# Issuing two memory-to-memory cache copies at another point of a hybrid attention and mLSTM layer

## The chip, the cores and the metric

The kernel runs on one core of one Trainium2 chip. The metric is the device time of one execution in microseconds (us). Three runs of the kernel before took 1609.83, 1607.42 and 1612.91 us, with a median of 1609.83. Beside them stands one profiled execution, from which every duration below is taken.

## The reference

One layer of a streaming model takes 256 prompt tokens and 64 sample tokens, each 2048 wide. The sample tokens attend to 512 cached keys and values. All numbers are float32. Cut to what is computed:

```
z = x @ w_in                                   # x 320 x 2048, w_in 2048 x 7184
attn: softmax(q k^T / 8 + bias) v, 16 heads, head norm
      sample: keys = [cache_k (512), new keys (64)], the same for values
      new_k_sample = [cache_k, k][-512:]       # 448 cached rows stay, 64 are new
      new_v_sample = [cache_v, v][-512:]
mLSTM: conv, gates, 8 heads of 128, head norm, * sigmoid(o)
x1 = layer_norm(alpha * x + concat(attn, mLSTM) @ w_out)
y  = layer_norm(alpha * x1 + (silu(x1 @ w_gate) * (x1 @ w_up)) @ w_down)
```

Of each of the two sample outputs, rows 0 to 447 are rows 64 to 511 of the cache, unchanged. These 448 rows of 1024 float32 are 1.84 MB for the keys and as much for the values. No engine computes on them: a DMA reads them from device memory and writes them to device memory.

## The kernel before

**Weights.** All matrices are cut into pieces of 512 KB (128 partitions x 1024 float32, mostly four blocks of 128 rows by 256 columns). `load_piece` (line 98) issues one DMA per piece on the queue of SyncE (SP), into one of four `raw` buffers. `split_piece` makes of it a high part on ScalarE (ACT, line 124, `hi`) and a low part on VectorE (DVE, line 125, `lo`); there are three buffers of each. TensorE (PE) then runs three passes per block (lines 174, 175, 177), which is 24 matmuls per piece of 256 columns. `run_plan` walks the list of pieces: it loads up to three pieces ahead and splits up to two ahead. Pieces are numbered here from 0; the first four make up the first strip of `w_in`.

**The opening.** The input `x` comes in four quarters (`xq`), each issued on SP just ahead of one of pieces 0 to 3. PE transposes each quarter (line 209), ACT and DVE split the result (`xhi`, line 210; `xlo`, line 211). Piece n multiplies quarter n. On ACT the high part of piece 4 stands ahead of the last quarter's `xhi`. After that quarter PE transposes the two tiles of small parameters (lines 234 and 235), and then runs piece 3.

**GpSimd's queue.** POOL issues the other DMAs: small parameters; a table of biases `fdram` (line 267); the cached keys and values that attention reads (`u`, lines 303 and 304, 512 KB each, into memory that the last two quarters of `x` held, so that they wait for their transposes); bias rows `tz` (line 312, 144 KB each); the mLSTM's states `cn` (line 584, 64 KB each, into the buffers of the small parameters, so that they wait for line 235). Between the static fills (line 289) and these loads, the program issues the two copies of the cache rows that stay (line 940).

**What sets the order.** Only the opening's PE, ACT and DVE work runs in the order of the text. Everywhere else a scheduler orders each engine's instructions by its own estimate of when their inputs will be there; an instruction without an input to wait for can be put far ahead of its place in the text. Each engine runs its list strictly in that order. POOL's DMAs take eight completion semaphores in turn, and each DMA waits until the last one with its semaphore has landed.

Of the kernel before, what the change touches and what calls it, by code (L numbers as in the profile page):

```python
# [23 lines left out]
SS = 64  # L24
T = SP + SS
PAST = 512
# [8 lines left out]
TOK = [(0, 128), (128, 128), (256, 64)]  # L35
# z columns
QA, KA, VA, QR, KR, VB, OB, IB = 0, 1024, 2048, 3072, 4096, 5120, 6144, 7168
# conv buffer: 3 past | prompt | 3 past | sample
CP0, CS0, CW = 3, 262, 326
# [4 lines left out]
class Piece:  # L44
    """A slice of a weight matrix and what is done with it."""

# [14 lines left out]
def _build(tc, nc, I, O, es):  # L61
# [12 lines left out]
    V, S, G, TE = nc.vector, nc.scalar, nc.gpsimd, nc.tensor  # L74

    # ---------------------------------------------------------------- input x
    xq = []
# [11 lines left out]

    # ------------------------------------------------------- weight streaming  # L90
    plan = []
    raws = []
    loaded = []
# [8 lines left out]
    def split_piece(between=None):  # L102
        i = len(loaded)
        pc, raw = plan[i], raws[i]
        raws[i] = None
        n = pc.nk * pc.ncol
        hi = wp.tile([P, PIECE], F32R, tag="hi", bufs=3, name="hi")
        if pc.perm:
            lo = None
            r3 = raw[:, 0:n].rearrange("p (k c) -> p k c", k=pc.nk)  # L110
            h3 = hi[:, 0:n].rearrange("p (k c) -> p k c", k=pc.nk)
            # high and low parts of the gates' columns side by side, for one pass with both
            S.copy(h3, r3)
            for d0, s0 in ((0, 112), (32, 120)):
                S.copy(h3[:, :, d0:d0 + 8], r3[:, :, s0:s0 + 8])
                V.tensor_tensor(out=h3[:, :, d0 + 64:d0 + 72], in0=r3[:, :, s0:s0 + 8],
                                in1=h3[:, :, d0:d0 + 8].bitcast(F32), op=ALU.subtract)
        else:
            lo = wp.tile([P, PIECE], F32R, tag="lo", bufs=3, name="lo")
            for j, m in enumerate((0, n // 2) if between else (0,)):  # L120
                if j:
                    between()
                cs = slice(m, m + n // 2 if between else n)
                S.copy(hi[:, cs], raw[:, cs])  # L124
                V.tensor_tensor(out=lo[:, cs], in0=raw[:, cs], in1=hi[:, cs].bitcast(F32),  # L125
                                op=ALU.subtract)
        loaded.append((hi, lo))
# [68 lines left out]

    # ------------------------------------------------------------ x transposed
    xhi = big.tile([P, KT, T], F32R, tag="A", bufs=2, name="xhi")
# [14 lines left out]

    # -------------------------------------------------------------- mixer pool
    mctx = tc.tile_pool(name="mx", bufs=1)
    mx = mctx.__enter__()

    # parameters that go along the partitions
    pcol = const.tile([P, P], F32, name="pcol")
# [28 lines left out]
    def rsqrt(out, u, n, m, tag):  # L248
        """out = u ** -0.5 by Newton's iteration; u and out are [n, m] in SBUF."""
        pool = const  # L250
# [8 lines left out]

    # ------------------------------------------------- relative position bias  # L260
    fdram = dp.tile([HA, 640], F32, name="fdram")
# [6 lines left out]

    # ------------------------------------------------------------- mix storage
    mixbuf = {}  # L270
# [8 lines left out]

    # ---------------------------------------------------------------- attention  # L280
    qbd = [const.tile([P, 5, P], F32, name="qbd%d" % i) for i in range(2)]
# [11 lines left out]
    def attn_loads(u):  # L293
        a = {}
# [4 lines left out]
        a["pT"] = u1[:, 1024:2432].rearrange("p (n c) -> p n c", c=P)  # L299
        # the second pair's probabilities take the place of the cached keys, then dead  # L300
        a["pt"] = [((0, u2[:, 1024:2240]),), ((960, u2[:, 2240:2496]), (0, u1[:, 0:960]))]
# [39 lines left out]
    def attn_gen(u, i):  # L341
        a = attn[u]
# [3 lines left out]
        cs = slice(i * P, (i + 1) * P)  # L346
        # keys and values by token, cached keys by feature
        for srcs, dst in ((vT, vtok), (kT, ktok)):
# [17 lines left out]
        yield  # L366
        # scores: cached keys | new keys, c1, c3, c0 | c2
        sa, sb, sc = w_tile(), w_tile(), w_tile()
# [25 lines left out]
        yield  # L394
        # probabilities by key
        pT = a["pT"]
# [57 lines left out]

    # -------------------------------------------------------------------- gates
    gate = {}
# [16 lines left out]
    def gates_done(ps):  # L473
# [9 lines left out]
        V.tensor_tensor(out=ig, in0=ig, in1=z[64:72, 0:T], op=ALU.add)  # L483
        # log_sigmoid(f) = min(f, 0) - log(1 + exp(-|f|))
        V.scalar_tensor_tensor(out=e, in0=f, scalar=-1.0, in1=f, op0=ALU.mult, op1=ALU.min)
# [16 lines left out]
        G.dma_start(out=gd_m, in_=nM)  # L502
        # exp(g - M_L), scaled as the keys need it
        wk = t8("ig2")
        for a, b in SEG:
            S.activation(wk[:, a:b], g[:, a:b], AF.Exp, bias=nM[:, b - 1:b])
        V.tensor_scalar(st[32:40, :], wk, KSC, None, ALU.mult)
        # exp(-m_t) = exp(-M - F)
        e1 = t8("e1")
        V.tensor_tensor(out=e1, in0=nM, in1=F, op=ALU.subtract)  # L510
        S.activation(e1, e1, AF.Exp)
        V.tensor_copy(st[64:72, :], e1)
        # exp(m_in - M), halved for the doubled queries
        wi = mx.tile([HB, SS], F32, tag="g8_wi", name="wi")
# [25 lines left out]

    # -------------------------------------------------------------------- mLSTM
    ml = {}
# [4 lines left out]
    def qk_done(u, kind, ps):  # L547
        for i in range(2):
# [14 lines left out]
            S.activation(th, acc, AF.Tanh, scale=0.5)  # L563
            # twice the SiLU
            y = mx.tile([P, CO], F32, tag="conv" + kind, bufs=2, name="cy")
# [11 lines left out]
    def mlstm_gen(h, i):  # L577
# [65 lines left out]
        G.tensor_copy(nnw[:, :, h], cw[:, :, 128])  # L643
        # h = num / max(|den|, exp(-m)), then the head's norm
        d = mx.tile([P, 3], F32, tag="d", bufs=2, name="d")
# [45 lines left out]
    def state_rows():  # L691
        """Rows of the conv and normaliser states, from the columns that were kept."""
        ps = w_tile()
# [9 lines left out]

    # ------------------------------------------------------ plan of the w_in part
    W = I["w_in"]
# [23 lines left out]

    # ------------------------------------------------------------- w_out and LN1  # L730
    def mix_rhs(k):
# [31 lines left out]
    def stat_gen(s, keep):  # L763
        """Token-major copies of two feature tiles of y: their statistics, and for the last
        norm the values too."""
        y, st = late["y"], late["st"]
# [22 lines left out]
    def sqrt_table(after):  # L789
        """Has the square root's table loaded before the norm's chain needs it."""  # L790
        d = const.tile([P, 1], F32, tag="sqd", name="sqd")
        S.activation(d, after, AF.Sqrt, bias=eps, scale=0.0)

    def norm_stats():
        """Mean and variance of the tokens, in columns for the three token tiles."""
        st = late["st"]
# [6 lines left out]
    def norm_rsqrt(mv):  # L803
# [5 lines left out]
        V.reciprocal(rn, sd)  # L809
        # one step of Newton's iteration  # L810
        a = const.tile([P, 3], F32, tag="rna", name="rna")
# [8 lines left out]

    # ----------------------------------------------------------------------- FFN
    x1 = {}
# [3 lines left out]

    # the first unit takes y * g with the columns g and b beside it; its norm is applied to
    # the products: W'((y - mu) r g + b) = r W'(y g) - mu r W'g + W'b
    def yg_rhs(k):
# [67 lines left out]
    def gate_up(u):  # L897
# [3 lines left out]
        if u == 0:  # L901
            # done with each quarter of the rows early, for the normed ones to replace them
            for pa, pb in zip(a, b):
                plan.extend((pa, pb))
        else:
            plan.extend(a + b)
# [16 lines left out]

    # --------------------------------------------------------------- the program
    for q in range(4):
# [12 lines left out]
    mix_tiles()  # L938
    for nm in ("k", "v"):
        G.dma_start(out=O["new_%s_sample" % nm][0:PAST - SS, :], in_=I["cache_attn_" + nm][SS:PAST, :])  # L940

    run_plan(n_in)
# [9 lines left out]
    G.dma_start(out=late["g2"], in_=ln2["g"].to_broadcast([P, DM]))  # L952
    # rows g, g, g, b, b as high, low, high, high, low parts
    gr = lp.tile([5, DM], F32, name="gr")
# [11 lines left out]

    # first norm, by feature
    def x1_gen():
# [21 lines left out]
        for c in range(KT):  # L990
            # in place of the rows that the first unit is done with
            if c % 2 == 0:
# [8 lines left out]
            V.tensor_tensor(out=lo, in0=y[:, c, :], in1=hi.bitcast(F32), op=ALU.subtract)  # L1001

    run_plan(len(plan))
    flush()

    # second norm, by token
    with tc.high_priority():
        for _ in stat_gen(7, (late["ytp"], late["yts"])):
# [5 lines left out]
                               op0=ALU.mult, op1=ALU.mult)  # L1014
        # rows -mean * r as high, high, low parts and ones, for -mean * r * g + b
        c5 = lp.tile([P, 3, 5], F32, name="c5")
# [55 lines left out]
```

## Time and profile before

| What | Value |
|---|---|
| median of three runs | 1609.83 us |
| span of the profiled execution (from its first to its last instruction; the profile gives no other time of it) | 1611.0 us |
| TensorE, share of the span | 98% |
| VectorE, ScalarE, GpSimd | 52%, 39%, 8% |
| mean granted TensorE clock | 0.990 |
| DMA, mean over the span | 148 GB/s |
| DMA, first fortieth of the span | 301 GB/s |

Each row of the tables is one group, wait or instruction; times within the span count from its start. In rows of the timeline the first number is the start, the second the duration, and the bracket at the end is the idle time of that engine just before, with what ended it. In the views of the DMA queues, q1 is the queue that SP fills and q0 the one that POOL fills; the row gives packets, MB and the share of the 16 DMA engines' time that the packets took.

### The profile page before, as it was taken

What the parts mean: (1) busy time and instruction counts of PE and PEld (TensorE: products, weight loads), DVE (VectorE), ACT (ScalarE), POOL (GpSimd) and SP (SyncE); (2) the same over time, 40 slices, a digit from 0 to 9 for tenths busy, and PEclk for the clock granted to TensorE, in tenths of its full rate; (3) what the DMA queues carried; (4) which work ended last, traced back from release to release, by engine and by line L of the source; (5) the groups of instructions that cost most, each with busy time, mean ns of one, the idle gap of its engine ahead of it and who ended that gap; (6) DMA issues with size and microseconds to landing.
All of it is one profiled execution on the core that took longest, in us unless ns stands there. A gap on an engine that the chain in (4) does not pass through costs nothing.

```text
span 1611.0 us, 26591 instructions
## 1 busy us (share of the span) xinstructions
PE 1579.4 (98%) x10906; PEld 1549.3 (96%) x10906; DVE 836.8 (52%) x1512; ACT 632.3 (39%) x972; POOL 123.4 (8%) x254
## 2 busy tenths in 40 slices
PE   5999999999999999999999999999999999999997
PEld 4999999999999999899999999999999999999996
DVE  3477585575665755853444444344444434444456
ACT  3356445444444533543333233333333333333332
POOL 3021111101000100400000000000000000000004
PEclk9999999999999999999999999999999999999997
DMA  9455444444344544354444444444444444444441
GB/s 301 152 158 153 144 144 147 149 144 128 121 128 128 176 142 143 105 169 145 151 150 148 154 145 155 145 155 146 148 153 146 156 144 154 148 150 151 148 141 66
DMA packets 225545, 238.99 MB, mean 148 GB/s; under 512 B 8683, under 2 KB 219819, under 8 KB 225227
## 3 DMA queue, kind: packets, MB, share of 16 engines
q1 hardware_dynamic: 220384, 220.23, 43.3%
q0 software_dynamic: 5040, 17.07, 3.3%
q8 instruction: 85, 1.39, 0.4%
q14 instruction: 36, 0.29, 0.1%
HBM read 230.85 MB, written 10.07 MB: 150 GB/s over the span
## 4 chain that ended last, share of the span: by engine, by line
PE 95%; DVE 2%; DMA 2%; issue 0%; ACT 0%; DVEq 0%; SPq 0%; ACTq 0%
PE mm L174 30%; PE mm L177 29%; PE mm L175 29%; DMA raw<-w_in 2%; PE w L419 1%; DVE lo L125 1%; PE w L771 1%; PE w L375 0%; PE w L399 0%; PE w L614 0%; DVE ytp L1034 0%; PE w L402 0%; PE w L352 0%; PE w L358 0%; PE w L377 0%; DVE t L998 0%
## 5 line engine op out<-in xcount | busy, mean ns | idle before, releaser
L125 DVE TENSOR_TENSOR lo<-raw,hi 128x1024 fp32r<-128x1024 f32 (+1 forms) x409 | 501.0, 1225 | 606.4 <-ACT hi L124 606.3
L124 ACT CAST hi<-raw 128x1024 fp32r<-128x1024 f32 (+1 forms) x409 | 428.1, 1047 | 754.8 <-PE mm L175 650.8
L177 PE MATMUL mm<-x1h,lo 128*128 128x320 f32 (+1 forms) x1408 | 436.5, 310 | 2.2 <-DVE lo L125 2.2
L174 PE MATMUL mm<-x1l,hi 128*128 128x320 f32 (+1 forms) x1408 | 435.6, 309 | 0.9 <-DVE np L844 0.9
L175 PE MATMUL mm<-x1h,hi 128*128 128x320 f32 (+1 forms) x1408 | 435.6, 309 | 0.0
L174 PE MATMUL mm<-xlo,hi 128*128 128x320 f32 x912 | 289.1, 317 | 0.0
L175 PE MATMUL mm<-xhi,hi 128*128 128x320 f32 x912 | 282.0, 309 | 0.0
L177 PE MATMUL mm<-xhi,lo 128*128 128x320 f32 x896 | 278.3, 311 | 0.5 <-DVE lo L125 0.5
L177 PEld LDWEIGHTS mm<-x1h,lo 128*128 128x128 f32 x1408 | 265.8, 189 | 2.6 <-DVE lo L125 2.5
L174 PEld LDWEIGHTS mm<-x1l,hi 128*128 128x128 f32 x1408 | 265.6, 189 | 1.3 <-DVE np L844 1.2
L175 PEld LDWEIGHTS mm<-x1h,hi 128*128 128x128 f32 x1408 | 265.4, 189 | 0.0
L174 PE MATMUL mm<-hl,hi 128*128 128x320 f32 x704 | 218.0, 310 | 0.0
L177 PE MATMUL mm<-hh,lo 128*128 128x320 f32 x704 | 217.5, 309 | 0.0
L175 PE MATMUL mm<-hh,hi 128*128 128x320 f32 x704 | 217.5, 309 | 0.0
L174 PEld LDWEIGHTS mm<-xlo,hi 128*128 128x128 f32 x912 | 172.4, 189 | 2.2
L175 PEld LDWEIGHTS mm<-xhi,hi 128*128 128x128 f32 x912 | 172.6, 189 | 0.0
L177 PEld LDWEIGHTS mm<-xhi,lo 128*128 128x128 f32 x896 | 169.4, 189 | 0.8 <-DVE lo L125 0.8
L175 PEld LDWEIGHTS mm<-hh,hi 128*128 128x128 f32 x704 | 132.2, 188 | 0.0
L174 PEld LDWEIGHTS mm<-hl,hi 128*128 128x128 f32 x704 | 132.1, 188 | 0.0
L177 PEld LDWEIGHTS mm<-hh,lo 128*128 128x128 f32 x704 | 132.1, 188 | 0.0
L779 POOL TENSOR_TENSOR ytp<-ytp,g 128x256 f32<-128x256 f32 x16 | 13.6, 875 | 894.6 <-ACT ytp L776 894.6
L888 DVE SCALAR_TENSOR_TENSOR y<-y,mm 128x320 f32<-128x320 f32 x96 | 46.5, 484 | 48.9 <-PE mm L177 48.6
(313 smaller groups left out, 1344.5 us busy)
## 6 DMA issues: line engine op xcount, KB each, us to landing
raw<-w_in SPq DMA_DIRECT2D x114, 512.0 KB, 3.5
raw<-w_ffn_gate SPq DMA_DIRECT2D x88, 512.0 KB, 3.5
raw<-w_ffn_up SPq DMA_DIRECT2D x88, 512.0 KB, 3.5
raw<-w_ffn_down SPq DMA_DIRECT2D x88, 512.0 KB, 3.3
raw<-w_out SPq DMA_DIRECT2D x32, 512.0 KB, 3.3
tz<-fdram POOLq DMA_DIRECT2D x16, 144.0 KB, 2.9
xq<-x_prompt SPq DMA_DIRECT2D x4, 512.0 KB, 8.6
u<-cache_attn_k POOLq DMA_DIRECT2D x4, 512.0 KB, 6.2
```

The source lines that it names most:

```text
L124: S.copy(hi[:, cs], raw[:, cs])
L125: V.tensor_tensor(out=lo[:, cs], in0=raw[:, cs], in1=hi[:, cs].bitcast(F32), op=ALU.subtract)
L174: TE.matmul(o, hi[:, sl], xl, start=st, stop=False)
L175: TE.matmul(o, hi[:, sl], xh, start=False, stop=en and pc.perm)
L177: TE.matmul(o, lo[:, sl], xh, start=False, stop=en)
L419: TE.matmul(ox[r, c * 64:(c + 1) * 64], pT[0:n, j, r], src[0:n, k, v0:v0 + 64], start=(m == 0), stop=(m == len(terms[c]) - 1))
L771: TE.transpose(dst[j][:, i * P:(i + 1) * P], y[:, 2 * s + i, t0:t0 + n], ident)
L779: G.tensor_tensor(out=keep[0][:, j, cs], in0=keep[0][:, j, cs], in1=late["g2"][:, cs], op=ALU.mult)
L888: V.scalar_tensor_tensor(out=y[:, c, :], in0=y[:, c, :], scalar=ALPHA if g == 0 else 1.0, in1=ps[i][:, 0:T], op0=ALU.mult, op1=ALU.add)
```

## The change

The loop that issues the two copies is taken from its place after `mix_tiles()` and put between two calls of `run_plan` in the feed-forward part: the plan now runs up to 32 pieces past the end of `w_out`, then come the copies, then the rest of the plan. The other differences of the file are comments that are gone, and shifted line numbers: lines 943 to 1001 are three lower in the changed kernel, those behind one higher, and the copies stand on line 1003.

```diff
     mix_tiles()
-    for nm in ("k", "v"):
-        G.dma_start(out=O["new_%s_sample" % nm][0:PAST - SS, :], in_=I["cache_attn_" + nm][SS:PAST, :])
-
     run_plan(n_in)
     flush()
     state_rows()
...
+    run_plan(n_out + 32)
+
+    for nm in ("k", "v"):
+        G.dma_start(out=O["new_%s_sample" % nm][0:PAST - SS, :], in_=I["cache_attn_" + nm][SS:PAST, :])
     run_plan(len(plan))
     flush()
```

What the scheduler makes of it is seen in the engines' lists. This is POOL's list of the kernel before, in the opening, from the last static fill (`vt1`) on: `u1` and `u2` are the cached keys and values that attention reads.

```order
L289 MEMSET vt1_87 128x3
L940 DMA new_k_sample<-cache_attn_k 32x14336
L940 DMA new_v_sample<-cache_attn_v 32x14336
L303 DMA u1_379<-cache_attn_k 128x4x256
L304 DMA u2_380<-cache_attn_v 128x4x256
L312 DMA tz_383<-fdram_81 64x576 x2
L312 DMA tz_386<-fdram_81 64x576 x2
L553 MEMSET craw_874 128x3
L494 MEMSET gst_1258 128x320
L584 DMA cn_1499<-state_mlstm_C 128x128
L584 DMA cn_1564<-state_mlstm_C 128x128
```

The same place in POOL's list of the changed kernel, from the last of six fills (lines 553, 494, 648 and 649) that now follow `vt1`:

```order
L649 MEMSET ss_1784 128x3
L1003 DMA new_k_sample<-cache_attn_k 32x14336
L303 DMA u1_377<-cache_attn_k 128x4x256
L304 DMA u2_378<-cache_attn_v 128x4x256
L312 DMA tz_381<-fdram_81 64x576 x2
L312 DMA tz_384<-fdram_81 64x576 x2
L584 DMA cn_1497<-state_mlstm_C 128x128
L584 DMA cn_1562<-state_mlstm_C 128x128
L1003 DMA new_v_sample<-cache_attn_v 32x14336
L312 DMA tz_1616<-fdram_81 64x576
```

The copies have no input to wait for, and the scheduler has put both into the opening again. The copy of the keys stands where it stood, behind six fills instead of ahead of them; the copy of the values has moved behind the loads of `u2`, `tz` and `cn`, and so behind the wait of `cn` for line 235. SP's list, which holds all loads of weights, is the same in both kernels.

PE's list changes in the first attention unit only. In the kernel before, the second head pair of that unit starts like this (352 and 353 are transposes of new values and keys, 358 of cached keys, 174 to 177 matmuls of the strips):

```order
L352 MATMUL w<-ident,vT 128x128 x2
L353 MATMUL w<-ident,vT 64x128
L174 MATMUL mm<-xlo,hi 128x320
L175 MATMUL mm<-xhi,hi 128x320
L177 MATMUL mm<-xhi,lo 128x320
L174 MATMUL mm<-xlo,hi 128x320
L352 MATMUL w<-ident,kT 128x128 x2
L353 MATMUL w<-ident,kT 64x128
L175 MATMUL mm<-xhi,hi 128x320
L177 MATMUL mm<-xhi,lo 128x320
L358 MATMUL w<-ident,u_379 128x128 x4
```

In the changed kernel the same place reads:

```order
L352 MATMUL w<-ident,vT 128x128 x2
L353 MATMUL w<-ident,vT 64x128
L352 MATMUL w<-ident,kT 128x128 x2
L353 MATMUL w<-ident,kT 64x128
L358 MATMUL w<-ident,u_377 128x128 x4
```

The strip's matmuls come behind the transposes instead of between them; units 1 to 3 have this second order in both kernels. ACT's and DVE's lists change in the same unit, and from there to the end no engine's list differs in more than line numbers.

## The prediction

> **What bounds the kernel now.** I read the page first, then PE's waits, then the chain of waits over the opening, then the two DMA queues by stretches. The page's first lines:
>
> ```profile
> span 1611.0 us, 26591 instructions
> PE 1579.4 (98%) x10906; PEld 1549.3 (96%) x10906; DVE 836.8 (52%) x1512; ACT 632.3 (39%) x972; POOL 123.4 (8%) x254
> ```
>
> PE is idle for 1611.0 - 1579.4 = 31.6 us, so no change of waits can win more, apart from what the clock gives. The list of PE's waits (us in total, times, longest) says where most of that lies:
>
> ```profile
> PE w L234 <- DVE xlo L211: 11.3, 1, 11.3
> PE w L1024 <- DVE c L1021: 5.4, 1, 5.4
> PE w L209 <- DMA xq<-x_prompt: 5.4, 1, 5.4
> PE mm L177 <- DVE lo L125: 2.7, 2, 2.2
> ```
>
> The second is the tail, the third the first load of `x`, and the fourth never exceeds 2.2 us. The change is near the first: one wait of 11.3 us in the opening. PE's timeline says when it began, and the chain of waits (start, us, what) what stands behind `xlo`:
>
> ```profile
> 28.40 0.31 PE L177 MATMUL mm<-xhi,lo 128*128 128x320 f32 x1
> ```
>
> ```profile
> 10.81 26.31 DMA raw<-w_in
> 37.23 1.05 ACT hi L124
> 38.30 1.23 DVE lo L125
> ...
> 39.98 0.47 PE w L234
> 40.46 0.28 PE w L235
> 40.74 0.56 PE mm L174
> 41.30 0.27 PE mm L175
> ...
> 44.22 0.15 PE mm L174
> ```
>
> PE's last matmul of piece 2 ends at 28.40 + 0.31 = 28.71, and the next instruction starts at 39.98: 11.27 us. The load of piece 4, issued at 10.81, took 26.31 us and landed at 37.12; its high part, which on ACT stands ahead of the last `xhi`, follows, and 2.86 us after the landing PE starts. So a stretch of a kernel that is PE-bound elsewhere is **bound by one DMA**. What held it is in the two queues; two rows each over 10 to 19 us and over 19 to 29 us, and one over 37 to 42 us:
>
> ```profile
> q1 hardware_dynamic: 2152, 2.75, 104.5%
> q0 software_dynamic: 203, 0.07, 4.2%
> q0 software_dynamic: 89, 3.69, 97.5%
> q1 hardware_dynamic: 126, 0.13, 4.0%
> q1 hardware_dynamic: 1396, 1.39, 95.0%
> ```
>
> From 10 to 19 us the loads from SP had the engines nearly alone (2.75 MB against 0.07). From 19 to 29 us POOL's queue moved 3.69 MB, which is the two copies (2 x 1.84), and the weights got 0.13 MB in 10 us. With POOL's queue nearly empty, from 37 to 42 us, they got 1.39 MB in 5 us, 0.278 MB per us. Between those, from 29 to 37 us, both queues moved:
>
> ```profile
> q0 software_dynamic: 452, 1.54, 63.1%
> q1 hardware_dynamic: 689, 0.68, 36.1%
> ```
>
> 1.54 + 0.68 = 2.22 MB in 8 us is the same 0.278 MB per us, two thirds of it for the attention's loads (`u` 2 x 0.52, `tz` 4 x 0.15 MB by their shapes). POOL's instructions show why these came so late:
>
> ```profile
> 14.52 0.51 POOL L940 DMA_DIRECT2D new_k_sample<-cache_attn_k  x1
> 15.03 0.51 POOL L940 DMA_DIRECT2D new_v_sample<-cache_attn_v  x1
> 21.20 0.80 POOL L303 DMA_DIRECT2D u<-cache_attn_k  x1 [5.66 <-PE w L209]
> 27.05 0.77 POOL L304 DMA_DIRECT2D u<-cache_attn_v  x1 [5.06 <-PE w L209]
> 27.81 2.16 POOL L312 DMA_DIRECT2D tz<-fdram  x4
> 40.76 1.10 POOL L584 DMA_DIRECT2D cn<-state_mlstm_C  x2 [10.38 <-PE w L235]
> ```
>
> ```profile
> new_k_sample<-cache_attn_k POOLq DMA_DIRECT2D x1, 1792.0 KB, 10.4
> new_v_sample<-cache_attn_v POOLq DMA_DIRECT2D x1, 1792.0 KB, 15.9
> ```
>
> The second fence is from the list of DMA issues: the copies landed 10.4 and 15.9 us after their issue, at 24.9 and 30.9: one behind the other, with about 5 us of the ten for each. The attention's loads queue behind both.
>
> **The change, part by part.** By POOL's list the change doesn't take the copies to the feed-forward part. It moves one of them, by a few instructions.
>
> *Keys.* Its copy stays ahead of `u`. Six fills come before it, one of which took 0.42 us and the others about what the last did:
>
> ```profile
> 29.95 0.42 POOL L494 MEMSET gst<- 128x320 f32 x1
> 41.94 0.13 POOL L649 MEMSET ss<- 128x3 f32 x1
> ```
>
> They overlap, so I add 0.7 us: it is issued at 15.2 instead of 14.52, and its 5 us run from 19.7 to 24.7.
>
> *Values, taken out.* The 5 us from 24.7 on are free. Up to about 29 only the first `u` (issued at 21.20, 0.52 MB) competes: the second is issued at 27.05, and POOL waits there for PE, not for the queue. Piece 4 lacks at most its whole 0.52 MB at 24.7. If the weights go first, it lands 0.52 / 0.278 = 1.9 us later, at 26.6; if `u` goes first, 3.7 us later, at 28.4. The other end lets every later load keep its place ahead of the weights; then the landing moves only by the copy's own 5 us, from 37.12 to 32.1. I take **28.5**, the case of `u` first, because the second `u` and `tz` can't move before they are issued, and their issue times come from PE. PE then starts at 28.5 + 2.86 = 31.4, its gap is 31.4 - 28.71 = 2.7 us, and 11.3 - 2.7 = **8.6 us** go (5.0 with the landing at 32.1, and 10.5 with it at 26.6).
>
> *The clock.* Once the opening is over, ACT splits a piece every 3.52 us, in PE's rhythm:
>
> ```profile
> 52.91 1.05 ACT L124 CAST hi<-raw 128x1024 fp32r<-128x1024 f32 x1 [2.47 <-PE mm L175]
> 56.43 1.05 ACT L124 CAST hi<-raw 128x1024 fp32r<-128x1024 f32 x1 [2.47 <-PE mm L175]
> ```
>
> That is 3.52 / 24 = 0.147 us per matmul. Behind the gap they are 0.27 us apart (the chain above): from 40.74 to 44.22 PE did 12 of them in 3.48 us instead of 1.76: **1.7 us** lost. When the clock fell is told by the row of a stretch (busy times, then the granted clock, the DMA share, GB/s):
>
> ```profile
> 33.00:35.00 2.00, 0.00 (x0) 0.00 (x0) 0.00 (x0) 0.00 (x0) 0.00 (x0) 0.71 1.07 334
> ```
>
> The slow rate is half the full one (0.27 to 0.147), and a mean of 0.71 between 1 and 0.5 means that it fell 0.84 us into this stretch, at 33.8, 5.1 us after PE stopped. A gap of 2.7 us stays under that, so I count the 1.7 us as won; with a gap over 5.1 us nothing of it is won. [...]
>
> *Values, put back.* This copy now waits behind `cn`, so for line 235. `cn` was issued 0.78 us after PE's restart and two take 1.10 us, so the copy is issued at 31.4 + 1.9 = 33.3. The copy of the keys moved its first data about 4.5 us after its issue (14.52 to 19, up to which POOL's queue moved only 0.07 MB), which gives 37.8 to 42.8 for this one, and in that time weights get almost nothing. What covers it is pieces in hand. From 28.5 to 37.8 the engines move 9.3 x 0.278 = 2.59 MB; the second `u`, `tz` and `cn` (2 x 0.07) take 1.24, and 1.35 MB are left, 2.6 pieces: 5, 6 and half of 7. PE needs 3.52 us per piece. From 31.4 + 0.8 on, pieces 3, 4, 5 and 6 keep it busy until 46.3; piece 7 must have landed 2.3 us (`hi` and `lo`) before, at 44.0. Its rest of 0.21 MB after 42.8 takes 0.8 us: 43.6. So it is just in time. If the cover fails altogether, it costs the 5 us; if not, nothing. I take **0.3**, near nothing, because the sum comes out in time, though barely. [...]
>
> *What is queued behind it.* The next instruction on POOL is a `tz`, which before stood idle until 85.43:
>
> ```profile
> 85.43 0.53 POOL L312 DMA_DIRECT2D tz<-fdram  x1 [43.37 <-DVE mxs L386]
> ```
>
> So nobody waits for a later issue, nor for the second `cn`, which now also waits for the keys' landing, long past.
>
> *The new order of attention unit 0.* Cost 0, since units 1 to 3 have that order already. Of equal stretches, that of unit 0 holds as many matmuls as that of unit 1, and PE is never idle in either:
>
> ```profile
> 74.00:124.00 50.00, 50.00 (x406) 47.70 (x405) 35.66 (x113) 26.33 (x59) 9.00 (x22) 1.00 0.50 152
> 189.00:239.00 50.00, 50.00 (x406) 47.79 (x405) 36.61 (x110) 23.35 (x51) 8.88 (x22) 1.00 0.49 152
> ```
>
> The bounds are 0 and 2.2 us, the longest wait of line 177 on `lo`.
>
> *The sum*: 1611.0 - 8.6 - 1.7 + 0.3 = 1601.0. The span lies 1.2 us above the runs' median of 1609.83, so a median of **1600** us is forecast.
>
> **The rivals.**
>
> A. *The gap shrinks only by the copy's own 5 us.* For: the attention's loads did take two thirds of the engines from 29 to 37. Against: their issue times don't move. The gap is 6.3 us, the clock falls, and the time is 1609.8 - 5.0 = 1604.8.
>
> B. *The clock halves sooner.* The gap is some 4 us and the clock falls in it: 7.3 us won, no 1.7, and 0.3 given back: 1602.8. For: one fall can't tell how the idle time is counted. Against: it took 5.1 us in the only long gap between matmuls. [...]
>
> C. *The copy of the values starves PE once it is moved.* It begins earlier than reckoned, before piece 6 is in hand, and PE waits its whole 5 us; with the clock kept, 1600 + 4.7 = 1604.7, and to 1606.4 with a second drop of the clock. For: the margin is 0.4 us.
>
> D. *Slower: the same, with a starvation as long as this copy's whole flight.* At `cn`, weights stand still for the 15.9 us that it took to land before, against 7.0 us (two pieces) in hand: 8.9 us of waiting and 1.7 of slow clock, beside a gain of only 5.0 as in A: 1609.8 + 5.6 = 1615.4. It is slower than before from a standstill of 10.3 us on (5.0 + 7.0 - 1.7). Against: 5 of those 15.9 us were the other copy's, and more was spent behind other loads.
>
> E. *Both copies leave the opening, as the text of the change has it.* Then the gap and the slow clock go: 1609.8 - 13.0 = 1596.8, if two copies amid the feed-forward part hide. POOL's list says otherwise.
>
> **How the numbers follow.** Forecast 0.55, A 0.15, B 0.11, C 0.12, D 0.04, E 0.03. The range 1596 to 1606 takes in all but D and the worst of C, with the spread of the runs. About 0.3%, 4.8 us, is what a measurement of this kernel can tell from no change. Faster by more: forecast, B, E and half of A, 0.77; within: C and the other half of A, 0.19; slower: D, 0.04.
>
> **What would show it.** Right: PE's wait at line 234 falls from 11.3 to 2 to 4 us; the load of piece 4 lands near 28.5; line 1003 shows two issues, near 15 and 33 us; no matmul at 0.27 us behind the gap; no new wait for `lo` from 35 to 50 us. Wrong: a copy issued in the feed-forward part, a gap over 5 us, or a PE wait on `raw` between 40 and 50 us.

## The result, and the profile after

| | before | after |
|---|---|---|
| median of four runs each, side by side | 1609.32 us (1607.42 to 1612.91) | 1601.93 us (1600.72 to 1603.01) |
| ratio, 95% interval | | 0.9949 (0.9935 to 0.9964) |
| span of the profiled execution | 1611.0 us | 1599.2 us |

The changed kernel is 7.4 us faster by the medians (0.46%); the ratio puts the gain at 0.51% (0.36 to 0.65). By the two profiled spans it is 11.8 us. These numbers differ because of which executions were profiled: every run of this kernel takes 1.7 to 2.1 us more than its span, so the profile of before belongs to a run of about 1612.9 us, the slowest of its four. That of after belongs to one of 1601.19.

The first two lines of the page of after:

```profile
span 1599.2 us, 26591 instructions
...
PE 1577.6 (99%) x10906; PEld 1547.5 (97%) x10906; DVE 836.4 (52%) x1512; ACT 631.9 (40%) x972; POOL 122.9 (8%) x254
```

PE's idle time fell from 31.6 to 1599.2 - 1577.6 = 21.6 us, by 10.0, and its busy time by 1.8. Both are in the opening. PE's waits of after (us in total, times, longest):

```profile
PE w L1025 <- DVE c L1022: 5.4, 1, 5.4
PE w L209 <- DMA xq<-x_prompt: 5.4, 1, 5.4
PE mm L177 <- DVE lo L125: 2.7, 2, 2.2
PE w L234 <- DVE xlo L211: 1.1, 1, 1.1
```

The wait ahead of line 234 fell from 11.3 to 1.1 us. The other rows stand as they stood. One short wait joins them: 0.2 us for a `hi` at 9.33 us, before either copy is issued, so it is not the copies' doing. The chain of waits through the opening of after (start, us, what):

```profile
11.50 15.55 DMA raw<-w_in
27.15 1.06 ACT hi L124
28.23 1.23 DVE lo L125
29.46 0.41 DVE xlo L211
29.92 0.33 PE w L234
30.24 0.19 PE w L235
30.44 0.34 PE mm L174
30.78 0.15 PE mm L175
```

Piece 4 is there at 11.50 + 15.55 = 27.05 us instead of 37.12, and PE starts 2.87 us later. Behind the gap the matmuls come at 0.15 us, not at 0.27: the slow clock is gone too. POOL's timeline of after (start, us, engine, line, operation; in brackets the idle time before and what ended it):

```profile
15.33 0.51 POOL L1003 DMA_DIRECT2D new_k_sample<-cache_attn_k  x1
...
30.54 1.10 POOL L584 DMA_DIRECT2D cn<-state_mlstm_C  x2 [0.49 <-PE w L235]
31.62 0.52 POOL L1003 DMA_DIRECT2D new_v_sample<-cache_attn_v  x1
```

Both copies are in the opening, at 15.33 and 31.62. Their packets show in the two queues of after, from 19 to 24 us, from 24 to 25.5, from 24 to 29, and from 37 to 42 (packets, MB, share of the 16 engines; two rows for each stretch):

```profile
q0 software_dynamic: 32, 1.84, 90.8%
q1 hardware_dynamic: 310, 0.31, 19.4%
q1 hardware_dynamic: 365, 0.36, 75.9%
q0 software_dynamic: 15, 0.00, 0.6%
q1 hardware_dynamic: 1066, 1.06, 66.8%
q0 software_dynamic: 160, 0.52, 29.3%
q0 software_dynamic: 49, 1.33, 66.0%
q1 hardware_dynamic: 224, 0.23, 13.6%
```

The first two rows are the copy of the keys, 32 packets of 57 KB, with 0.31 MB of weights in the same stretch. Of these, 0.29 MB passed before 20 us, while the large packets were only starting; from 20 to 24.2 us it was 16 packets of 1 KB, beside the 16 large ones that started then. The next four are the five microseconds that the change frees: 1.06 MB of weights beside the first `u` of 0.52, with the weights alone up to 25.5 us. In the last two the copy of the values does to the weights what that of the keys did, but nobody waits for them by then. That is seen in PE's waits from 30 to 70 us (one row, which is the end of the gap above) and in ACT's timeline:

```profile
43.99 1.05 ACT L124 CAST hi<-raw 128x1024 fp32r<-128x1024 f32 x1 [5.05 <-DMA raw<-w_in]
45.46 1.05 ACT L124 CAST hi<-raw 128x1024 fp32r<-128x1024 f32 x1 [0.42 <-DMA raw<-w_in]
...
48.13 1.05 ACT L124 CAST hi<-raw 128x1024 fp32r<-128x1024 f32 x1 [1.23 <-PE mm L175]
```

ACT waits 5.05 us for piece 8, and from 48.13 on it waits for PE again, as in the steady part. PE takes a piece every 3.52 us from 30.44 on and so comes to piece 8 at about 48.0, which is an estimate. Piece 8 is split about 2.3 us after 43.99, at 46.3. So 1.7 us were to spare.

### The profile page after: what moved, and what is told of

Its sections match the earlier page's. It is cut to its first block, busy times and chain, and to the rows that moved or that the text cites. A ratio compares the mean times of both kernels' runs of the same rounds, so it can differ in the third digit from the quotient of the medians.

```text
span 1599.2 us, 26591 instructions
## 1 busy us (share of the span) xinstructions
PE 1577.6 (99%) x10906; PEld 1547.5 (97%) x10906; DVE 836.4 (52%) x1512; ACT 631.9 (40%) x972; POOL 122.9 (8%) x254
## 4 chain that ended last, share of the span: by engine, by line
PE 95%; DVE 2%; DMA 1%; issue 0%; SPq 0%; ACT 0%; DVEq 0%; ACTq 0%
PE mm L174 30%; PE mm L177 30%; PE mm L175 29%; PE w L419 1%; DMA raw<-w_in 1%; PE w L771 1%; DVE lo L125 1%; DMA xq<-x_sample 1%; PE w L375 0%; PE w L399 0%; PE w L614 0%; DVE ytp L1035 0%; PE w L352 0%; PE w L402 0%; PE w L358 0%; PE w L377 0%
```

## The experiments

The theory: the whole gain is the gap ahead of line 234 with the slow clock behind it; taking either copy out from between 19 and 30 us is enough; where it goes costs nothing as long as the pieces in hand last. The rivals: the gain is the spread of runs; it is due to the new order in attention unit 0 or to a true move into the feed-forward part; the moved copy takes back a part. Three chips served, one for each group of runs, and every ratio is to runs of before on the same chip.

### Before again, and one copy moved at a time

The kernel before, run again as if it were a change:

> The kernel before once more, to see how far its own gap in front of line 234 moves from run to run. Theory (the gap is set by the two copies in front of piece 4, and its length varies with how the packets fall): the ratio's interval contains 1, the gap lies between 6 and 12 us, and the runs scatter by some 4 us. Rival (the gap is fixed, and the runs scatter for another reason): the gap is 11.3 us again within 0.5 us, whatever the time.

Measured: 1612.13 us (1604.51 to 1614.42, 10 runs), ratio 1.0004 (0.9989 to 1.0019). Its profiled execution, of 1610.04 us and a span of 1608.1, has another gap than the one shown with the prediction. Of its chain of waits:

```profile
11.47 22.62 DMA raw<-w_in
34.19 1.05 ACT hi L124
...
36.95 0.47 PE w L234
```

Its DMA queues over 9 us of the copies, from 19.75 to 28.75 us, and behind them those of the kernel before that the prediction showed, from 19.5 to 28.5:

```profile
q0 software_dynamic: 64, 2.75, 84.6%
q1 hardware_dynamic: 64, 0.07, 2.1%
q0 software_dynamic: 64, 2.75, 83.7%
q1 hardware_dynamic: 64, 0.06, 2.2%
```

Piece 4 landed at 34.09 instead of 37.12, and the gap is 7.6 us (its wait row says so too). So **the gap of before is not a constant**, and before scatters over 9.9 us here while after stayed within 2.9 in its ten runs, four beside the result and six with the last pair below. But once the large packets run, the counts are the same in both profiles: 64 packets of POOL's queue (48 of them of 57 KB) and 64 of weights. What differs is what had passed by then and how fast the loads came after it: the first large packet started at 19.48 us here and at 19.03 in the other, and by 34 us 4424 packets had passed in SP's queue instead of 4330. At the 57 to 83 packets a microsecond that passed there from 33 to 36 us, those 94 packets are some 1.5 us (an estimate). The rest of the 3.0 us between the two landings stays open.

Only the copy of the values moved:

```diff
-    for nm in ("k", "v"):
+    for nm in ("k",):
         G.dma_start(out=O["new_%s_sample" % nm][0:PAST - SS, :], ...)
...
+    run_plan(n_out + 32)
+    for nm in ("v",):
+        G.dma_start(out=O["new_%s_sample" % nm][0:PAST - SS, :], ...)
```

> Only the copy of the values is taken to the later place in the text; the copy of the keys stays in its place, ahead of the six fills. In POOL's list the values' copy again comes behind cn. Theory (the whole gain is the values' copy leaving the front of piece 4): PE's wait at line 234 is 1 to 3 us, the slow matmuls behind it are gone, and the time is that of the changed kernel within 2 us. Rival (moving the keys' copy behind six fills, or the new order of attention unit 0, has a share): less than three quarters of the gain.

Measured: 1602.22 us (1600.14 to 1603.14), 0.9944 (0.9927 to 0.9961), a gap of 2.15 us and no slow matmul behind it. It does what the change does. The mirror of it, with only the copy of the keys moved:

> Mirror of the one before: only the copy of the keys is moved, the copy of the values stays in front. Theory (it matters only that one copy of two stands in front of piece 4, not which): the same wait of 1 to 3 us at line 234 and the same time as the changed kernel within 2 us. Rival (the keys' copy collides with the attention's load of the cached keys, or the order of the two matters): the wait stays above 5 us.

Measured: 1601.17 us (1599.61 to 1604.76), 0.9943 (0.9923 to 0.9963). It doesn't matter which copy stays. The profiled execution of this run is the slowest of its four runs, and holds a surprise. The gap is 2.97 us and PE starts again at 32.02. Two stretches of 3.41 us (busy us of PE, PEld, DVE, ACT, POOL, the granted clock, the DMA share, GB/s):

```profile
29.67:33.09 3.42, 1.07 (x6) 0.89 (x7) 2.75 (x6) 2.89 (x6) 1.49 (x5) 1.00 1.10 348
33.09:36.50 3.41, 3.41 (x15) 3.41 (x14) 1.86 (x7) 0.83 (x2) 1.29 (x7) 0.50 1.04 218
```

The clock fell at 33.09, when PE had been at work for a microsecond, and 0.27 us per matmul lasted until 36.5. More on this below.

### No copy in the opening

The copies left out:

> Both copies are left out, so rows 0 to 447 of the two sample outputs stay unwritten. Theory (after the change only about 1 us of the gap is left to win, and the moved copy costs nothing): the wait at line 234 is 0 to 1.5 us and the time is within 2 us of the changed kernel. Rival (the copy that stays in front, or the moved one, still costs several us): 3 us or more below the changed kernel.

Measured: 1600.73 us (1600.26 to 1601.05), 0.9937 (0.9921 to 0.9952), and no wait at line 234 at all. This is what can be had by moving the copies: after, which did not run beside it, is 1.2 us above it. Next, the copies at the point that the change's text names. They are held there until GpSimd's last operation of the first norm is done:

```diff
-            G.tensor_tensor(out=t1, in0=y[:, c, :], in1=mu, op=ALU.subtract)
+            late["last"] = G.tensor_tensor(out=t1, in0=y[:, c, :], in1=mu, op=ALU.subtract)
...
-    for nm in ("k", "v"):
-        G.dma_start(out=O["new_%s_sample" % nm][0:PAST - SS, :], ...)
...
+    run_plan(n_out + 32)
+    with tc.issue_after(late["last"].ins):
+        for nm in ("k", "v"):
+            G.dma_start(out=O["new_%s_sample" % nm][0:PAST - SS, :], ...)
```

> What the text of the change says: both copies are held, by an edge in the scheduler, behind the last of line 997's subtractions on POOL, and so are issued in the feed-forward part, near 680 us. Theory (10 us of large packets there are covered by three pieces in hand, but barely): the opening's gap is 0 to 1.5 us, PE waits 0 to 4 us for a piece in the feed-forward part, and the time is within 4 us of the changed kernel. Rival (steady weight traffic has no slack): PE waits 8 us or more there and the gain is mostly gone.

Measured: 1601.95 us (1601.21 to 1602.11), 0.9934 (0.9914 to 0.9955). They are issued at 670.2 and 670.7. Its queues from 671 to 683 us, and PE's only wait from 670 to 700:

```profile
q0 software_dynamic: 96, 3.67, 87.6%
q1 hardware_dynamic: 255, 0.26, 7.7%
```

```profile
PE mm L174 <- DVE np L844: 2.4, 1, 2.4
```

The weights get 0.26 MB in 12 us there, and PE waits for none of them; its one wait is for VectorE's part of the norm. That wait is 0.9 us in the profiles of before and after, and 2.5 in a second profile of the changed kernel (the run again, below), which has no copy there; so its length varies without the copies. By these times a true move is worth no more than the one that the scheduler made.

### How long a standstill is hidden

Both copies held behind the load of the states, where after has one:

```diff
+        ld = G.dma_start(out=cn[:, 0:128], in_=I["state_mlstm_C"][h])
+        if h == 1:
+            late["cn"] = ld
...
+    with tc.issue_after(late["cn"].ins):
         for nm in ("k", "v"):
```

> Both copies are held behind the second cn on POOL, where the changed kernel has only that of the values. Theory (in the changed kernel the moved copy's five us of standstill used up nearly all pieces in hand, since ACT waited 5.05 us for a piece and PE 0.2): twice the standstill costs PE 3 to 7 us between 40 and 55 us, so the time lies 2 to 6 us above the changed kernel's. Rival (there is more slack): PE waits under 1 us there, and the time equals the changed kernel's.

Measured: 1602.44 us (1600.59 to 1603.11), 0.9936 (0.9918 to 0.9955). The wait that was expected did not come. (The 0.2 us of PE's waiting that the expectation counted is the wait at 9.33 us, ahead of the copies.) Its large packets ran from 33.1 to 44.9 us, and the row of that stretch (length, then busy us of PE, PEld, DVE, ACT, POOL, the granted clock, the DMA share, GB/s) is

```profile
33.00:45.00 12.00, 12.00 (x83) 12.00 (x83) 3.68 (x3) 4.01 (x5) 0.00 (x0) 1.00 1.01 377
```

PE was busy for all of the 12 us. With the front free, the loads had run ahead, and the pieces in hand were more than had been counted. Where the cover ends was still open, so a third copy, of the cached keys into scratch memory, went ahead of these two:

```diff
+        scr = dp.tile([PAST - SS, 1024], F32, name="scr")
+        G.dma_start(out=scr, in_=I["cache_attn_k"][SS:PAST, :])
         for nm in ("k", "v"):
```

> As in the run with both copies behind the states' load, with a third copy of 1.84 MB of the cached keys into scratch memory issued just ahead of them, so that a standstill of the weights three copies long stands in one piece. In the run with two, the large packets ran from 33.1 to 44.9 us, piece 9 landed at 45.4 and was split by about 50.1, and TensorE, which needed it at about 50.5, did not wait. A third copy takes 5 to 6 us more. Theory 1 (the copies cost nothing only while pieces in hand last): the large packets end at 50 to 51 us, piece 9 lands near 51, TensorE waits 4 to 6 us for hi or lo at 50 to 56 us, 14 to 24 matmuls behind it run at the slow clock (2 to 3 us), and the time is 5 to 9 us above that run: 1607 to 1611. Theory 2 (copies behind cn are hidden whatever their length, since the loads of weights still get their share): no new wait, within 1.5 us of 1602.

Measured: 1607.73 us (1605.36 to 1610.97, 10 runs), 0.9977 (0.9965 to 0.9989). PE's waits from 30 to 75 us, and of the stretches behind them two rows:

```profile
PE mm L174 <- ACT hi L124: 5.4, 1, 5.4
PE mm L177 <- DVE lo L125: 0.4, 1, 0.4
```

```profile
46.00:48.00 2.00, 0.65 (x5) 0.39 (x3) 0.00 (x0) 0.00 (x0) 0.00 (x0) 1.00 0.39 118
...
54.00:56.00 2.00, 2.00 (x9) 2.00 (x9) 1.92 (x3) 1.17 (x2) 0.00 (x0) 0.50 0.77 212
```

The large packets ran from 32.4 to 50.5, 18.1 us. PE stopped at 46.65, waited 5.39 + 0.36 us, and worked at half the clock until 57.0, for 15 matmuls. So some 18.1 - 5.8 = 12.3 us of standstill are hidden at this place (an estimate), and what goes beyond is paid, with the slow clock on top. After's standstill, 5.9 us by its large packets (36.3 to 42.2), is well inside.

### The size of the packets

The copies where they stood before, but cut into rows of 4 KB instead of 57 KB:

```diff
     for nm in ("k", "v"):
-        G.dma_start(out=O["new_%s_sample" % nm][0:PAST - SS, :], in_=I["cache_attn_" + nm][SS:PAST, :])
+        G.dma_start(out=O["new_%s_sample" % nm][0:PAST - SS, :].rearrange("(n p) c -> p n c", p=P // 2),
+                    in_=I["cache_attn_" + nm][SS:PAST, :].rearrange("(n p) c -> p n c", p=P // 2))
```

> The copies stay where they were before the change, but are written as 64 x 7 rows of 4 KB instead of 32 rows of 57 KB: the same bytes in smaller packets. Theory (the weights starve because each turn of POOL's queue is a packet of 57 KB): the weights get a fifth of the traffic meanwhile, piece 4 lands by 27 to 33 us, and the wait at line 234 falls to 1 to 6 us. Rival (only the bytes matter): the wait stays near that of the kernel before, 8 to 12 us.

Measured: 1604.14 us (1602.44 to 1609.1, 7 runs), 0.9951 (0.9935 to 0.9966). The profiled execution is again the slowest of its runs. Its queues from 20 to 28 us, and PE's waits from 28 to 60:

```profile
q0 software_dynamic: 653, 2.61, 79.9%
q1 hardware_dynamic: 654, 0.65, 23.0%
```

```profile
PE mm L174 <- ACT hi L124: 2.8, 1, 2.8
PE mm L177 <- DVE lo L125: 0.7, 1, 0.7
PE w L234 <- DVE xlo L211: 0.5, 1, 0.5
```

Again as many packets pass in one queue as in the other: 653 and 654. With packets of 4 KB the weights so got 0.65 MB in 8 us, a fifth of the bytes, where the large packets left them 0.06 or 0.07 in 9, and the gap at line 234 fell to 0.5 us without moving anything, below the range that the theory gave. But the bytes are the same and the copies last longer (12.4 and 18.9 us from issue to landing, against 10.4 and 15.9), so in this execution waits of 2.8 and 0.7 us came later instead, at piece 6, and the clock was halved behind them from 44.4 to 51.2 us. What its other runs, 4 to 7 us faster, lost there was not traced. **Here the size of the packets set who was starved; the bytes still had to go somewhere that is covered.**

### A version without the second read

Attention has the cached keys and values in on-chip memory anyway. Here their rows are stored from there, in every attention unit, and the copies fall away:

```diff
+        if i == 0:
+            hs = slice(u * 256, (u + 1) * 256)
+            for nm, src in (("k", ck), ("v", cv)):
+                o = O["new_%s_sample" % nm]
+                G.dma_start(out=o[0:SS, hs], in_=src[SS:P, 0, :])
+                G.dma_start(out=o[SS:PAST - SS, hs].rearrange("(n p) c -> p n c", p=P),
+                            in_=src[:, 1:4, :])
```

> The memory-to-memory copies are dropped; the rows that stay are written, unit by unit, from the cached keys and values that attention has loaded anyway. Theory: as without copies, a wait at line 234 of 0 to 1.5 us, no standstill later, and the time of the changed kernel or up to 2 us less. Rival (the stores delay POOL's other loads, or the buffers' reuse waits for them): a new wait of ACT or DVE in the attention units and 2 us or more above the changed kernel.

Measured: 1600.38 us (1600.16 to 1600.6), 0.9926 (0.9909 to 0.9942), no wait at line 234. To see whether it beats the changed kernel, both ran on one chip:

> The changed kernel again, on the chip of the next run, to compare the two. Both theories: 1600.5 to 1603, with a gap of 1 to 3 us ahead of line 234 and no slow matmuls behind it, or, if the gap comes out above 2.2 us, up to 14 slow matmuls (1.7 us).

> The rows that stay are stored from the keys and values that attention has read, without copies from memory to memory; against the changed kernel on the same chip. Theory 1 (the changed kernel still loses its gap of about 1 us at line 234 and now and then a phase of slow clock): 1 to 2.5 us less than the changed kernel. Theory 2 (the first difference, 1600.4 against 1601.9, was the spread of chips and runs): less than 0.5 us between the two.

Measured: the changed kernel 1601.97 us (1600.49 to 1603.33, 6 runs), with a gap of 1.28 us and no slow matmul behind it; this one 1600.18 (1599.73 to 1603.76, 6 runs). The medians are 1.8 us apart, as they were 1.6 apart in the runs before, but the ranges overlap, and the ratios 0.9939 (0.9923 to 0.9954) and 0.9934 (0.9916 to 0.9951) can't be told apart. Of the 3.0 us between the two profiled spans, about 1.5 are the wait in the first norm that varies (2.45 us against 0.93), where neither version has a copy. It is faster than before; that it beats the changed kernel is likely, but not shown.

## Why the prediction was right, and where its steps were off

The forecast was 1600.0 us, and the time was 1601.93. By its steps:

- **The copies stay in the opening, and only the values' moves.** Right: they are issued at 15.33 and 31.62 (15.2 and 33.3 forecast).
- **The gap.** The mechanism was right, and the term was too small: 11.27 - 1.12 = 10.2 us went instead of 8.6. Piece 4 landed at 27.05, not at 28.5. I had let the first `u` go ahead of the weights. But its packets began only at 25.6, 4.3 us after its issue at 21.28: the delay of about 4.5 us from issue to data, which I had counted for the copy of the values, I had not counted for `u`. Up to 25.5 the weights had the engines alone, and of the 1.58 MB until 29 us they got 1.06. The bound of 26.6, with the weights first, was nearer. The 2.86 us from landing to PE's start held.
- **The slow clock.** 1.7 us were forecast and went. But the reason, that the clock falls only 5.1 us after PE stops, is wrong: it fell 4.0 us after PE had stopped, behind a gap of 2.97 us, in the run with only the keys moved. With the 1.12 us of after it held. Had the gap been the 2.7 us that I forecast, the 1.7 us could have been lost, so this term came out partly by luck. Rival B (the clock falls sooner) was nearer to how the clock behaves, and even a gap shorter than its 4 us was enough.
- **The copy of the values, put back.** Hidden, as forecast; the term of 0.3 was 0. Its data began at 36.3, 4.7 us after its issue (4.5 forecast). It was not "just in time": piece 8 was split 1.7 us ahead of its use, because the earlier landing of piece 4 moved the loads behind it forward too. The cover was under-counted: with two copies in a row 11.8 us of standstill cost nothing, and by the run with three some 12.3 us can be hidden, where rival D had allowed for 7.0 us in hand. D's mechanism is real, as the third copy shows, but its price begins later than I put it, and in after the large packets ran for 5.9 us, not for 15.9. Rival C, the starved PE, needs a standstill of more than some 12 us at this place. Weights got almost nothing beside it, as counted: 39 packets with 0.04 MB from 37 to 41 us, beside 36 of POOL's queue with 1.33 MB, 23 of them of 57 KB. (Of the 126 packets of weights from 19 to 29 us of before, 50 passed before 19.5 us, while the first large ones were starting.)
- **Attention unit 0.** Cost 0, as forecast: from its first line 352 to its first line 532 it takes 65.93 us before and 66.01 after.
- **The sum.** The profile of after shows 10.2 + 1.7 = 11.9 us won, and the spans differ by 11.8.
- **From span to median.** This step failed. I took the span for 1.2 us above the median run and subtracted that. A run's time is about 1.9 us more than its span, and the profiled execution of before was the slowest of its four runs, 3.6 us above their median, with a gap at the long end (11.3 us; in another profile 7.6, with a span 2.9 us shorter). So of the 11.8 us some 3.6 belong to that one execution, and 0.7 more came from after's profiled run lying below its own median: 11.8 - 3.6 - 0.7 = 7.5 against the 7.4 measured. The sum stood 1.8 us above the span that came (1601.0 against 1599.2), and this step subtracted 1.2 where 1601.93 - 1599.2 = 2.7 was to be added, 3.9 too low: half of the second error was covered by the first, and that the median came within 2 us of the forecast is in part luck.

That the gain is the gap and the clock is shown by the runs without copies and with either copy moved. Rival E, both copies truly in the feed-forward part, would have given the same time (1601.95), not 1596.8: its price was worked out from the same profiled execution and has the same fault. What stays open is what decides, from one execution to the next, how much of the weights is through before the large packets start and how fast the rest lands behind them, and so how long the gap of before is.

## What to carry to other kernels

Each of the two copies took 0.51 us of POOL for its issue and nothing else of any engine, and together they still held up PE for 11.3 us: look at the size of such a copy's packets and at what else is queued while they run, and put it where several pieces are in hand, or cut it into smaller rows. When you count the packets that pass beside it, start the count where its first packet starts. When the order is a scheduler's, read from its list where an instruction without inputs really ends up; the place in the text decided little here. The stall made here by a race of two queues differed between executions (11.3 us in one profile of before, 7.6 in the other), so its length in one profile was no measure of the median: look at the spread of the runs first.

## What was not expected of the hardware

**Short gaps and the clock.** In the profile of before, PE waits 2.21 us for `lo` in the norm, until 678.31, and 0.63 us after it is back at work its clock is halved; behind the gap of 2.15 us in the run with only the values moved the clock stayed full. Two stretches there, and two of the run with only the values moved, around its gap of 2.15 us (length, PE, PEld, DVE, ACT, POOL, clock, DMA share, GB/s):

```profile
675.53:678.94 3.41, 1.21 (x8) 0.94 (x8) 3.41 (x3) 3.09 (x6) 3.15 (x3) 1.00 0.01 3
678.94:682.35 3.41, 3.41 (x15) 3.41 (x14) 3.41 (x7) 2.00 (x5) 1.86 (x3) 0.50 0.49 156
27.07:30.48 3.41, 1.84 (x12) 1.58 (x11) 2.01 (x2) 2.17 (x5) 3.23 (x7) 1.00 1.02 341
30.48:33.89 3.41, 2.83 (x18) 2.65 (x19) 3.41 (x11) 1.37 (x3) 1.84 (x8) 1.00 1.05 275
```

The clock is full throughout the wait in the norm, falls at 678.94 and is back at 682.35. In the opening of before it is halved from 33.82 to 44.06, which is 10.24 us or 3 x 3.413; from there to 678.94 it is full, 634.88 us or 186 x 3.4133. It is halved for 6.83 us with three copies and with small packets, and for 3.41 here and in the run with only the keys moved. The stretches are cut on that grid. PE's work in the stretch ahead of the fall was 1.21 us here, and 1.07 with only the keys moved, as shown above. The gap of 2.15 us lies across two stretches, with 1.84 and 2.83 us of work, and cost nothing. In the profiles of before and after the clock left full speed five times: in before behind stretches with 0, 1.21 and 1.52 us of work (until 33.82, 678.94 and 1593.71), in after behind 1.51 and 0.63 (until 668.09 and 1582.86). Behind one with 1.72 us, from 26.99 to 30.41 of before, it stayed full. A fall for one stretch cost about 13 matmuls at 0.27 us, 13 x 0.12 = 1.6 us (an estimate). In long gaps the clock fell 5.1 us into the one of 11.27 (before), 3.5 into the one of 5.39 (three copies) and 1.9 into the one of 7.60 (before again). No run here varied the phase of a gap on purpose, so what makes the clock fall is not shown.

**Packets of two queues.** Once the copies' packets ran, 64 packets of POOL's queue and 64 of weights passed in 9 us of each of the two profiles of before, and 653 and 654 in 8 us with packets of 4 KB: one for one in all three stretches. A packet of the copies carried 57 KB in the first two and 4 KB in the third, one of weights 1 KB. So the packets were shared evenly there and the bytes were not: 2.75 MB against 0.06 or 0.07, and 2.61 against 0.65.
